# The input's chunked transfers on SyncE's queue, and a recurrence that passes its state every 128 tokens

## The chip, the cores and the metric

The kernel runs on one core of one Trainium2 chip. The metric is the device time of one execution in microseconds (us). Its engines are TensorE (PE in the profile, with its weight loads as PEld), VectorE (DVE), ScalarE (ACT), GpSimd (POOL) and SyncE (SP). SyncE, ScalarE and GpSimd each have a queue from which they hand transfers to the 16 DMA engines.

## What is computed

One forward pass of a stack of four layers over 512 tokens of width 1024: a state-space mixer (S5) and a short convolution, each followed by a SwiGLU, then dilated attention and a gated recurrence (HGRN2), each followed by a squared-ReLU MLP. The change touches the first mixer's loads and the last mixer's recurrence. Cut to those two:

```python
def s5_mixer(h, a_re, a_im, log_step, b_re, b_im, c_re, c_im, d, w_out):
    u = h.reshape(bsz, seqlen, 64, 16)              # 64 groups of 16 channels, 64 complex states each
    abr, abi = mag * cos(li * dt), mag * sin(li * dt)
    ...
    _, _, xr, xi = lax.associative_scan(_ssm_combine, (a_r, a_i, bu_re, bu_im), axis=1)
    y = einsum('ghp,blgp->blgh', c_re, xr) - einsum('ghp,blgp->blgh', c_im, xi)
    ...

def hgrn2_mixer(x, w_in, w_out, norm_g, lb):        # 8 heads of 128, chunks of C = 64 tokens
    q, key, log_f, v = chunks(q, K), chunks(key, K), chunks(log_f, K), chunks(v, V)
    b = cumsum(log_f, axis=3)
    q_dec, k_dec = q * exp(b), key * exp(-b)
    a = where(causal, einsum('bhcid,bhcjd->bhcij', q_dec, k_dec), 0.0)
    o_intra = einsum('bhcij,bhcje->bhcie', a, v)
    b_last = b[:, :, :, -1:, :]
    kv = einsum('bhcjd,bhcje->bhcde', key * exp(b_last - b), v)
    # state_{c+1} = exp(b_last_c) * state_c + kv_c ; states[c] is the state before chunk c
    o_inter = einsum('bhcid,cbhde->bhcie', q_dec, states)
    o = o_intra + o_inter                           # then a norm over each head, and a projection
```

## The kernel before

Activations lie transposed: `xT` holds 8 blocks of 128 channels by 512 tokens. A large product is the sum of three float32r products (`whi*hhi`, `whi*hlo`, `wlo*hhi`: L832 to L834 over 512 tokens, L1567 to L1569 for `v`); ScalarE makes `whi` from each loaded weight tile (L785) and VectorE `wlo` (L786). These products fill TensorE for most of the run. The order of the instructions on each engine is set when the program is built, by a scheduler that looks at the dependences and at its own estimate of each duration; so a change in one place can shift the instructions around it. Each engine then runs its list in that order and waits where an operand is late.

**The start.** `s5()` builds the first mixer's tables. ScalarE first issues the transfers of constants, of the mixer's `b` and `c` (`crow`, L182) and of `x` (L185: two transfers of 1 MB each, in which every second 128-channel block of 8 consecutive tokens goes to one partition). SyncE issues the loads of `w_ada`, 1 MB each (L232, three buffers; 20 in this stage), from which TensorE computes the modulation vectors (L239). What the tables need: VectorE derives an angle `t1y` and a magnitude; ScalarE takes its sine and cosine (`sn` L431, `cs` L433); VectorE makes the powers `pw_re`, `pw_im`; TensorE transposes `crow` (L553) and ScalarE copies it to `c` (L554); GpSimd multiplies powers and `c` into output tables `ft` (L539 to L541), and later makes `sr`, `d` and two of the intermediates `w1t` (L517). `ORDER`, a string, gives the order in which these steps are handed to the scheduler: `A` is one modulation load with its products, `K` is `setup`, `Q` the sum of squares of `x`. The first large products start at about 203 us.

**The recurrence.** `hgrn_pair(b, first)` does two heads; four pairs follow each other. Its three products are handed out before the two heads' own steps. For a head, VectorE scans the log decay (L1581), ScalarE takes three exponentials, and VectorE makes `qd` (L1587), `kd` (L1592) and the key `kk` scaled to the chunk's end (L1597). TensorE transposes `kk` (L1600), ScalarE copies it to `kt` (L1602), and TensorE makes the four 128x128 score blocks (L1605), of which VectorE keeps the causal part inside each 64-token chunk (L1607). The loop over eight chunks of 64 tokens then adds for each its scores times `v` (L1615, once per two chunks), the state times `qd` (L1617) and the chunk's `kt` times `v` (L1620, which reads 64 of the 128 partitions); VectorE updates the state `hst` in between (L1625). A plain float32 product takes two matrix instructions, so the profile counts two for each (112 for L1620's 56, x8 for four of L1605); the transposes count one. A norm over the head follows (L1628 to L1636).

## Time and profile before

| | us |
|---|---|
| median of 3 runs | 2822.16 |
| lowest and highest | 2821.14, 2823.73 |
| the profiled execution, device time | 2826.84 |
| its span, first to last instruction | 2825.1 |

The profile is of one execution, whose own time is 1.74 us above its span. Each row of a timeline gives a start in us from the span's first instruction and the time it took; "ACTq" and "SPq" are the queues of ScalarE and SyncE, whose rows are the issuing of transfers. A matrix instruction's own duration contains the depth of the pipeline, so what one costs in a row of them is the distance from its start to the next one's.

### The profile page before, as it was taken

The numbers are of one execution on the slowest core, as the hardware profiler recorded it, in microseconds if no ns is written. First come the engines' busy times: TensorE is split into PE (matmuls) and PEld (weight loads), VectorE is DVE, ScalarE is ACT, GpSimd is POOL, SyncE is SP. The second block draws the span as 40 slices with busy tenths as digits, with TensorE's granted clock in tenths as the row PEclk, the third lists the DMA queues.
The fourth block names the chain that finished last, engine by engine and source line by source line (L and its number), as shares of the span: only waits on it lengthen the run. The fifth ranks groups of instructions, "written<-read, shape, count | busy, mean of one in ns | idle before, by whom it ended". The sixth has DMA issues, their size and how long they took to land.

```text
span 2825.1 us, 37880 instructions
## 1 busy us (share of the span) xinstructions
PE 2750.9 (97%) x15516; PEld 2308.2 (82%) x15516; DVE 1570.5 (56%) x2819; ACT 1081.8 (38%) x1872; POOL 127.3 (5%) x122
## 2 busy tenths in 40 slices
PE   5899999999999999999999999999999999999998
PEld 3568978889788888898888888888888888988887
DVE  7867755547455333475545555754437656744435
ACT  4553422224233222253434434442324676532221
POOL 6520000000000000000000000000000000000000
PEclk9989999999999999999999999999999999999999
DMA  8446445433323232343323333133223212223221
GB/s 217 145 130 222 151 147 164 149 119 104 98 97 105 80 103 94 108 117 93 102 75 98 97 87 87 46 103 100 91 79 110 90 46 75 76 90 101 87 82 60
DMA packets 300866, 298.40 MB, mean 106 GB/s; under 512 B 9732, under 2 KB 287108, under 8 KB 300692
## 3 DMA queue, kind: packets, MB, share of 16 engines
q1 hardware_dynamic: 288532, 277.27, 31.2%
q10 hardware_dynamic: 9824, 12.34, 1.9%
q0 software_dynamic: 2336, 6.36, 1.0%
q8 instruction: 122, 2.00, 0.3%
q14 instruction: 52, 0.43, 0.0%
HBM read 278.90 MB, written 2.10 MB: 99 GB/s over the span
## 4 chain that ended last, share of the span: by engine, by line
PE 91%; ACT 3%; DVE 3%; POOL 2%; issue 1%; ACTq 1%; DMA 0%; SPq 0%; DVEq 0%; POOLq 0%
PE ps_mm L832 25%; PE ps_mm L833 24%; PE ps_mm L834 24%; PE ps_mm L845 2%; PE ps_mm L846 2%; PE ps_mm L847 2%; PE ps_sc L1300 1%; PE ps_pt L1327 1%; PE ps_kv L1620 1%; PE ps_b L670 1%; POOL ft L541 1%; POOL ft L540 1%; PE ps_mm L1202 1%; PE ps_mm L1204 1%; PE ps_mm L1203 1%
## 5 line engine op out<-in xcount | busy, mean ns | idle before, releaser
L832 PE MATMUL ps_mm<-hhi,whi 128*128 128x512 f32 (+1 forms) x2064 | 797.5, 386 | 0.0
L833 PE MATMUL ps_mm<-hlo,whi 128*128 128x512 f32 (+1 forms) x2064 | 791.5, 383 | 0.4 <-DVE hlo L357 0.4
L834 PE MATMUL ps_mm<-hhi,wlo 128*128 128x512 f32 (+1 forms) x2064 | 790.6, 383 | 0.2 <-DVE wlo L786 0.2
L785 ACT CAST whi<-raw 128x1024 fp32r<-128x1024 f32 (+1 forms) x428 | 413.8, 990 | 824.8 <-PE ps_mm L833 637.0
L786 DVE TENSOR_TENSOR wlo<-raw,whi 128x1024 fp32r<-128x1024 f32 (+1 forms) x428 | 485.6, 1151 | 390.3 <-ACT whi L785 358.7
L832 PEld LDWEIGHTS ps_mm<-hhi,whi 128*128 128x128 f32 x2064 | 387.5, 188 | 84.9 <-issue 3.1
L834 PEld LDWEIGHTS ps_mm<-hhi,wlo 128*128 128x128 f32 x2064 | 387.3, 188 | 83.0 <-DVE wlo L786 0.6
L833 PEld LDWEIGHTS ps_mm<-hlo,whi 128*128 128x128 f32 x2064 | 387.7, 188 | 80.4 <-DVE hlo L357 0.9
L833 PE MATMUL ps_mm<-hidl,whi 128*128 128x512 f32 (+1 forms) x1184 | 421.1, 356 | 0.3 <-DVE hidl L357 0.3
L832 PE MATMUL ps_mm<-hidh,whi 128*128 128x512 f32 (+1 forms) x1184 | 420.3, 355 | 0.4 <-ACT hidh L356 0.4
L834 PE MATMUL ps_mm<-hidh,wlo 128*128 128x512 f32 (+1 forms) x1184 | 420.4, 355 | 0.0
L833 PEld LDWEIGHTS ps_mm<-hidl,whi 128*128 128x128 f32 x1184 | 223.5, 189 | 32.1 <-DVE hidl L357 0.5
L832 PEld LDWEIGHTS ps_mm<-hidh,whi 128*128 128x128 f32 x1184 | 223.3, 189 | 32.2 <-ACT hidh L356 0.8
L834 PEld LDWEIGHTS ps_mm<-hidh,wlo 128*128 128x128 f32 x1184 | 223.5, 189 | 31.0
L1151 DVE TENSOR_TENSOR xT<-xT,ps_mm 128x512 f32<-128x512 f32 (+1 forms) x144 | 78.6, 552 | 133.9 <-PE ps_mm L834 132.6
L846 PE MATMUL ps_mm<-hhi,wlo 128*128 128x256 f32 x448 | 124.1, 279 | 0.0
L847 PE MATMUL ps_mm<-hlo,whi 128*128 128x256 f32 x448 | 123.8, 279 | 0.4 <-DVE hlo L357 0.4
L845 PE MATMUL ps_mm<-hhi,whi 128*128 128x256 f32 x448 | 123.3, 280 | 0.7 <-ACT hq L1546 0.6
L356 ACT CAST hidh<-silu 128x512 fp32r<-128x512 f32 (+1 forms) x124 | 68.9, 565 | 129.2 <-DVE silu L978 86.3
L939 DVE SCALAR_TENSOR_TENSOR xT<-ps_mm,mods,xT 128x512 f32<-128x512 f32 (+1 forms) x104 | 64.8, 626 | 93.6 <-PE ps_mm L834 93.3
L277 DVE SCALAR_TENSOR_TENSOR ada_acc<-raw,c_act,ada_acc 128x256 f32<-128x256 f32 x196 | 93.6, 483 | 4.9
L1251 POOL DMA_DIRECT2D qsw<-qc x48 | 23.4, 492 | 1583.7 <-ACT qc L1240 1569.5
(403 smaller groups left out, 3379.5 us busy)
## 6 DMA issues: line engine op xcount, KB each, us to landing
raw<-in_w_ada_dram SPq DMA_DIRECT2D x48, 1024.0 KB, 5.4
raw<-in_w_ffn_in_dram SPq DMA_DIRECT2D x44, 1024.0 KB, 5.1
raw<-in_ffn_w_up_dram SPq DMA_DIRECT2D x32, 1024.0 KB, 5.5
raw<-in_attn_w_in_dram SPq DMA_DIRECT2D x48, 512.0 KB, 5.2
raw<-in_ffn_w_down_dram SPq DMA_DIRECT2D x32, 768.0 KB, 4.3
raw<-in_w_ffn_out_dram SPq DMA_DIRECT2D x24, 768.0 KB, 4.3
raw<-in_conv_w_in_dram SPq DMA_DIRECT2D x12, 1024.0 KB, 5.3
raw<-in_attn_w_in_dram SPq DMA_DIRECT2D x12, 1024.0 KB, 5.1
```

The lines of the kernel that those rows point to most:

```text
L277: V.scalar_tensor_tensor(ac, raw[:, k, :], c_act[:, k:k + 1], ac, op0=OP.mult, op1=OP.add)
L356: A.copy(hi, src)
L785: A.copy(hi[:, sl], raw[:, sl])
L786: V.tensor_tensor(lo[:, sl], raw[:, sl], hi[:, sl].bitcast(F32), op=OP.subtract)
L832: T.matmul(ps[:, 0:n], hi[:, k, cs], h, start=(k == 0), stop=False)
L833: T.matmul(ps[:, 0:n], hi[:, k, cs], l, start=False, stop=False)
L834: T.matmul(ps[:, 0:n], lo[:, k, cs], h, start=False, stop=(k == nk - 1))
L845: T.matmul(p[:, 0:n], hi[:, k, cs], h, start=(k == 0), stop=False)
L846: T.matmul(p[:, 0:n], lo[:, k, cs], h, start=False, stop=False)
L847: T.matmul(p[:, 0:n], hi[:, k, cs], l, start=False, stop=(k == nk - 1))
L939: V.scalar_tensor_tensor(x, ps, gcol[:, m:m + 1], x, op0=OP.mult, op1=OP.add)
L1151: V.tensor_tensor(x, x, ps, op=OP.add)
```

## The change

The two transfers of `x` move out of the straight list at the head of the program into `load_chunks`, which `setup` (step `K0` of `ORDER`, after two `A` steps) calls, and SyncE issues them instead of ScalarE. In the recurrence the state is passed every 128 tokens. `join0` and `join1` hold, for each 128 tokens, the decay over its second half, two ones, and the decay over its first half; with them `kk` is scaled on to the end of the 128 tokens (`kl`) and `qd` back to their beginning (`qf`). The scores between the two halves come from an extra product of 64x64 (`kk` of the first half with `qd` of the second), which overwrites a quarter of each score block, and the mask keeps all of `qi <= kj`. What is left of the loop: three `kv` products over 128 partitions each into one bank, three state updates, four score products and three state products over 128 columns.

```diff
--- before.py
+++ after.py
@@ -58,7 +58,7 @@
     ct["selA"] = np.concatenate([(qi == 4 * np.arange(32)[None] + r).astype(f) for r in range(4)], 1)
     ct["qbm"] = (qi // 32 == np.arange(4)[None]).astype(f)
     ct["selB"] = np.concatenate([(kj == 4 * (qi % 32) + r).astype(f) for r in range(4)], 1)
-    tril = ((qi // 64 == kj // 64) & (qi <= kj)).astype(np.int32)
+    tril = (qi <= kj).astype(np.int32)
     ct["tri"] = tril.view(f)
     ct["rst"] = one * (np.arange(512) % 64 != 0).astype(f)[None]
     offs, cols, o = {}, [], 0
@@ -181,9 +181,12 @@
     for i, nm in enumerate(("ssm_c_re", "ssm_c_im")):
         nc.scalar.dma_start(crow[:, :, i, :], dap(a[nm], 0, [[64, 128], [64 * 128, 8], [1, 64]]))
 
-    for s in range(2):
-        nc.scalar.dma_start(xc[64 * s:64 * s + 64].rearrange("p l i j -> p (l i) j"),
-                            dap(a["x"], s * 128, [[8 * D, 64], [256, 32], [1, 128]]))
+    def load_chunks():
+
+        for s in range(2):
+            nc.sync.dma_start(xc[64 * s:64 * s + 64].rearrange("p l i j -> p (l i) j"),
+                              dap(a["x"], s * 128, [[8 * D, 64], [256, 32], [1, 128]]))
+
     nc.gpsimd.dma_start(drow, dap(a["ssm_d"], 0, [[0, 16], [16, 64], [1, 16]]))
 
     ident = C("ident")
@@ -567,6 +570,7 @@
 
 
         def setup(_):
+            load_chunks()
 
             P.memset(X, 0.0)
             P.tensor_tensor(X[0:16], drow, C("e")[0:16, None, :].to_broadcast([16, 64, 16]), op=OP.mult)
@@ -1532,10 +1536,20 @@
         t = hp.tile([128, 4, 128], F32, name=f"aT{i}", bufs=1)
         P.memset(t, 0.0)
         aT.append(t)
+
+    joins = []
+    for i in range(2):
+        t = hp.tile([128, 4, 4], F32, name=f"join{i}", bufs=1)
+        P.memset(t, 1.0)
+        joins.append(t)
     load_consts(hp, "tri", "rst", bufs=1)
     tri = C("tri").bitcast(I32)
     rst = C("rst")
     hid = {}
+
+    def nt_tile(shape):
+        t = sm.tile([128, 2, 256], F32, name="nt", tag="nt", bufs=3).rearrange("p k t -> p (k t)")
+        return t if len(shape) == 2 else t.rearrange("p (c i) -> p c i", c=shape[1])
 
     def hgrn_pair(b, first):
         nonlocal psG
@@ -1580,9 +1594,11 @@
             bb = t.rearrange("p (c i) -> p c i", c=8)
             V.tensor_tensor_scan(bf, rst, t, 0.0, op0=OP.mult, op1=OP.add)
             ex = hp.tile([128, S], F32, name="hx", bufs=2)
-            dec = hp.tile([128, 8], F32, name="hdec")
+            jn = joins[m % 2]
+            be = t.rearrange("p (q f i) -> p q f i", q=4, f=2)
             A.activation(ex, bf, AF.Exp)
-            A.activation(dec, bb[:, :, 63], AF.Exp)
+            A.activation(jn[:, :, 0], be[:, :, 1, 63], AF.Exp)
+            A.activation(jn[:, :, 3], be[:, :, 0, 63], AF.Exp)
             qd = qs[:, s]
             V.tensor_tensor(qd, qs[:, s], ex, op=OP.mult)
             ex2 = hp.tile([128, S], F32, name="hx", bufs=2)
@@ -1590,40 +1606,50 @@
             V.tensor_scalar(ke[:, s], ke[:, s], olb[:, m:m + 1], None, op0=OP.mult)
             kd = ex2
             V.tensor_tensor(kd, ke[:, s], ex2, op=OP.mult)
-            ex3 = hp.tile([128, 8, 64], F32, name="hx", bufs=2)
+            ex3 = nt_tile([128, 8, 64])
             V.tensor_tensor(ex3, bb[:, :, 63:64].to_broadcast([128, 8, 64]), bb, op=OP.subtract)
             A.activation(ex3, ex3, AF.Exp)
             kk = ex3.rearrange("p c i -> p (c i)")
             V.tensor_tensor(kk, kk, ke[:, s], op=OP.mult)
+
+            def joined(dst, src, c0):
+                h4 = lambda x: x.rearrange("p (q f i) -> p q f i", q=4, f=2)
+                V.tensor_tensor(h4(dst), h4(src), jn[:, :, c0:c0 + 2, None].to_broadcast([128, 4, 2, 64]), op=OP.mult)
+
+
+            kl = ke[:, s]
+            joined(kl, kk, 0)
+            qf = nt_tile([128, S])
+            joined(qf, qd, 2)
+            dec = hp.tile([128, 4], F32, name="hdec")
+            V.tensor_tensor(dec, jn[:, :, 0], jn[:, :, 3], op=OP.mult)
             kps = pst("ka", (128, 4, 128))
             for t_ in range(4):
-                T.transpose(kps[:, t_], kk[:, nat_tile(t_)], ident)
-            kt = ke[:, s].rearrange("p (q e) -> p q e", q=4)
-            A.copy(kt, kps)
+                T.transpose(kps[:, t_], kl[:, nat_tile(t_)], ident)
             aps = pst("ka", (128, 4, 128))
             for t_ in range(4):
                 T.matmul(aps[:, t_], kd[:, nat_tile(t_)], qd[:, nat_tile(t_)], start=True, stop=True)
+                o = t_ * 128
+                T.matmul(aps[0:64, t_, 64:128], kk[:, o:o + 64], qd[:, o + 64:o + 128], start=True, stop=True)
+            kt = ke[:, s].rearrange("p (q e) -> p q e", q=4)
+            A.copy(kt, kps)
             aa = aT[m % 2]
             V.copy_predicated(aa, tri[:, None, :].to_broadcast([128, 4, 128]), aps)
             es = slice(s * 128, s * 128 + 128)
+            kv = pst("kv")[:, 0:384].rearrange("p (q e) -> p q e", q=3)
+            for t_ in range(3):
+                T.matmul(kv[:, t_], kt[:, t_], v[:, t_, es], start=True, stop=True)
+            sts = hp.tile([128, 3, 128], F32, name="hst", bufs=1)
+            for t_ in range(3):
+                if t_ == 0:
+                    V.tensor_copy(sts[:, 0], kv[:, 0])
+                else:
+                    V.scalar_tensor_tensor(sts[:, t_], sts[:, t_ - 1], dec[:, t_:t_ + 1], kv[:, t_], op0=OP.mult, op1=OP.add)
             ops = pst("ho", (128, 4, 128))
-            st = None
-            for c in range(8):
-                t_, hf = c // 2, c % 2
-                rows = slice(64 * hf, 64 * hf + 64)
-                if hf == 0:
-                    T.matmul(ops[:, t_], v[:, t_, es], aa[:, t_], start=True, stop=False)
-                if c:
-                    T.matmul(ops[:, t_, rows], st, qd[:, c * 64:c * 64 + 64], start=False, stop=(hf == 1))
-                if c < 7:
-                    kv = pst("kv")[:, 0:128]
-                    T.matmul(kv, kt[rows, t_], v[rows, t_, es], start=True, stop=True)
-                    ns = hp.tile([128, 128], F32, name="hst", bufs=3)
-                    if st is None:
-                        V.tensor_copy(ns, kv)
-                    else:
-                        V.scalar_tensor_tensor(ns, st, dec[:, c:c + 1], kv, op0=OP.mult, op1=OP.add)
-                    st = ns
+            for t_ in range(4):
+                T.matmul(ops[:, t_], v[:, t_, es], aa[:, t_], start=True, stop=(t_ == 0))
+                if t_:
+                    T.matmul(ops[:, t_], sts[:, t_ - 1], qf[:, nat_tile(t_)], start=False, stop=True)
             ot = sg[:, s]
             A.copy(ot, ops.rearrange("p q t -> p (q t)"))
             sq = hp.tile([128, S], F32, name="hx", bufs=2)
```

On SyncE's list the rows that follow the six small loads are these before (`raw` is a buffer of `w_ada`, `TT` a table that is filled from `X`):

```order
L158 DMA vrow_82<-in_c_dram 8x128
L158 DMA vrow_82<-in_norm_g_dram 16x128
L158 DMA vrow_82<-in_b_ada_dram 96x128
L232 DMA raw<-in_w_ada_dram 128x8x256 x13
L665 DMA TT_255<-X 16x256
L232 DMA raw<-in_w_ada_dram 128x8x256
L665 DMA TT_254<-X 16x256
L665 DMA TT_254<-X 32x256
L665 DMA TT_254<-X 48x256
L665 DMA TT_254<-X 64x256
```

and in the changed kernel these, where the two transfers of `x` stand behind two of `w_ada`, and the first full group of `TT` stands behind eleven of `w_ada` instead of fourteen:

```order
L158 DMA vrow_82<-in_c_dram 8x128
L158 DMA vrow_82<-in_norm_g_dram 16x128
L158 DMA vrow_82<-in_b_ada_dram 96x128
L235 DMA raw<-in_w_ada_dram 128x8x256 x2
L187 DMA xT<-in_x_dram 64x32x128 x2
L235 DMA raw<-in_w_ada_dram 128x8x256 x9
L669 DMA TT_252<-X 16x256
L669 DMA TT_252<-X 32x256
L669 DMA TT_252<-X 48x256
L669 DMA TT_252<-X 64x256
L669 DMA TT_252<-X 80x256
L669 DMA TT_252<-X 96x256
```

On ScalarE's list the first instructions that are not transfers stand before like this (`vcol` holds small vectors, `c_act` the activated condition, `IC` an identity):

```order
L182 DMA crow<-in_ssm_c_im_dram 128x8x64
L185 DMA xT<-in_x_dram 64x32x128 x2
L166 ACT_TABLE_LOAD
L166 COPY vcol_123<-ps_a 128x120
L431 ACT_TABLE_LOAD
L431 ACTIVATE sn<-t1y 128x64
L388 ACT_TABLE_LOAD
L388 ACTIVATE c_act<-vcol_123 128x8
L432 ACTIVATE ab<-t1y 128x64
L574 COPY IC_256<-cst_ident 128x8x128
L433 ACTIVATE cs<-ab,cst_sws 128x64
```

In the changed kernel the `x` row is gone, and the rest keeps its order:

```order
L182 DMA crow<-in_ssm_c_im_dram 128x8x64
L166 ACT_TABLE_LOAD
L166 COPY vcol_121<-ps_a 128x120
L434 ACT_TABLE_LOAD
L434 ACTIVATE sn<-t1y 128x64
L391 ACT_TABLE_LOAD
L391 ACTIVATE c_act<-vcol_121 128x8
L435 ACTIVATE ab<-t1y 128x64
L578 COPY IC_254<-cst_ident 128x8x128
L436 ACTIVATE cs<-ab,cst_sws 128x64
```

On TensorE's list the first head of the recurrence begins like this before (`ps_ka` are transposes and scores, `ps_kv` the products for the state, `ps_ho` the output, `ps_mm` the large products of the next pair):

```order
L1600 MATMUL ps_ka<-cst_ident,hx 128x128 x4
L1605 MATMUL ps_ka<-hq,hx 128x128 x4
L832 MATMUL ps_mm<-hhi,whi 128x512
L833 MATMUL ps_mm<-hlo,whi 128x512
L834 MATMUL ps_mm<-hhi,wlo 128x512
L1620 MATMUL ps_kv<-hv,hk 128x128
L832 MATMUL ps_mm<-hhi,whi 128x512
L833 MATMUL ps_mm<-hlo,whi 128x512
L834 MATMUL ps_mm<-hhi,wlo 128x512
L832 MATMUL ps_mm<-hhi,whi 128x512
L833 MATMUL ps_mm<-hlo,whi 128x512
L1615 MATMUL ps_ho<-aT_17301,hv 128x128
```

In the changed kernel the scores alternate with the 64x64 products, the three `kv` stand together, and one large product stands between scores and `kv` where there were three:

```order
L1628 MATMUL ps_ka<-cst_ident,hk 128x128 x4
L1631 MATMUL ps_ka<-hq,hx 128x128
L1633 MATMUL ps_ka<-hq,nt 64x64
L1631 MATMUL ps_ka<-hq,hx 128x128
L1633 MATMUL ps_ka<-hq,nt 64x64
L1631 MATMUL ps_ka<-hq,hx 128x128
L1633 MATMUL ps_ka<-hq,nt 64x64
L1631 MATMUL ps_ka<-hq,hx 128x128
L1633 MATMUL ps_ka<-hq,nt 64x64
L836 MATMUL ps_mm<-hhi,whi 128x512
L1641 MATMUL ps_kv<-hv,hk 128x128 x3
```

Between the transposes of a pair's first head and those of its second there are 66 large products of `ps_mm` before and 26 in the changed kernel; the others stand behind the second head (30 before, 70 now), since the next pair's products are as many as they were.

## Rows read from the trace of the kernel before

**Rows 1.** The page: the span, and the chain that ended last by engine.

```profile
span 2825.1 us, 37880 instructions
...
PE 91%; ACT 3%; DVE 3%; POOL 2%; issue 1%; ACTq 1%; DMA 0%; SPq 0%; DVEq 0%; POOLq 0%
```

**Rows 2.** Chain that ended last, first 90 us: start, us, what.

```profile
22.60 1.28 ACT L166
...
32.38 0.34 DVE pw_re L424
...
83.81 1.98 POOL w1t L517
```

**Rows 3.** Timeline of ScalarE's queue: start, us; x2 merges two instructions.

```profile
6.88 1.80 ACTq L182 DMA_DIRECT2D crow<-in_ssm_c_im_dram  x1
...
8.72 13.85 ACTq L185 DMA_DIRECT2D xT<-in_x_dram  x2
```

**Rows 4.** DMA issues, first 140 us: KB each, median us from issue to landing.

```profile
xT<-in_x_dram ACTq DMA_DIRECT2D x2, 1024.0 KB, 20.9
```

**Rows 5.** Timeline of the start on VectorE, TensorE, ScalarE and GpSimd.

```profile
14.43 0.19 DVE L420 TENSOR_SCALAR t1y<-t1y 128x64 f32<-128x64 f32 x1
...
23.42 1.30 PE L553 MATMUL ps_a<-cst_ident,crow 128*128 128x128 f32 x5 [12.90 <-DMA crow<-in_ssm_c_im_dram]
...
25.46 0.26 ACT L431 ACTIVATE sn<-t1y 128x64 f32<-128x64 f32 x1
...
31.54 1.27 ACT L554 ACTIVATE c<-ps_a,cst_sws 128x512 f32<-128x512 f32 x2
...
32.86 9.91 POOL L539 TENSOR_TENSOR ft<-c,pw_re 128x512 f32<-128x512 f32 x8 [5.36 <-DVE tq L424]
```

**Rows 6.** Busy time of each engine by stretch; PEclk is the granted clock.

```profile
100.00:200.00 100.00, 86.00 (x655) 62.65 (x654) 74.04 (x91) 56.87 (x118) 40.96 (x29) 0.85 0.36 118
...
170.00:180.00 10.00, 10.00 (x52) 8.19 (x53) 2.58 (x4) 5.48 (x8) 3.19 (x3) 0.52 0.01 3
...
2199.00:2431.00 232.00, 225.95 (x1386) 193.78 (x1387) 135.18 (x243) 151.69 (x216) 0.00 (x0) 1.00 0.19 60
```

**Rows 7.** Timeline of TensorE in the first recurrent head: start, us.

```profile
2223.65 0.66 PE L1600 MATMUL ps_ka<-cst_ident,hx 128*128 128x128 f32 x4 [1.39 <-DVE hx L1597]
...
2224.14 1.06 PE L1605 MATMUL ps_ka<-hq,hx 128*128 128x128 f32 x8
...
2224.96 0.48 PE L832 MATMUL ps_mm<-hhi,whi 128*128 128x512 f32 x1
...
2229.68 0.33 PE L1617 MATMUL ps_ho<-hq,hst 128*128 128x64 f32 x2
...
2229.93 0.48 PE L1620 MATMUL ps_kv<-hv,hk 64*128 64x128 f32 x2
...
2230.35 0.50 PE L832 MATMUL ps_mm<-hhi,whi 128*128 128x512 f32 x1
...
2230.68 0.40 PE L833 MATMUL ps_mm<-hlo,whi 128*128 128x512 f32 x1
...
2230.92 0.39 PE L834 MATMUL ps_mm<-hhi,wlo 128*128 128x512 f32 x1
...
2231.82 0.49 PE L1615 MATMUL ps_ho<-aT,hv 128*128 128x128 f32 x2
...
2232.07 0.48 PE L832 MATMUL ps_mm<-hhi,whi 128*128 128x512 f32 x1
```

**Rows 8.** Line L1620: what ended TensorE's idle time (us, times).

```profile
  ACT hk L1602: 5.0, 6
```

**Rows 9.** VectorE groups, 2199 to 2431 us: xcount | busy us, mean ns | idle.

```profile
L786 DVE TENSOR_TENSOR wlo<-raw,whi 128x1024 fp32r<-128x1024 f32 x19 | 22.8, 1216 | 1.5 <-ACT whi L785 1.5
...
L1625 DVE SCALAR_TENSOR_TENSOR hst<-hst,hdec,ps_kv 128x128 f32<-128x128 f32 x48 | 16.6, 347 | 36.1 <-PE ps_kv L1620 35.7
...
L1592 DVE TENSOR_TENSOR hx<-hk,hx 128x512 f32<-128x512 f32 x8 | 5.5, 692 | 2.8 <-ACT hx L1589 2.8
```


## The prediction

> **What bounds the kernel now.** I read the page first. The chain that ended last lies on TensorE for 91% of the span [rows 1]; there, time goes only if TensorE's own work shrinks or something that it waits for comes earlier. The change touches two places, so I read each by itself.
>
> The start: the chain of waits runs for its first 32 us over ScalarE's queue, then VectorE, then GpSimd until 85.8 us [rows 2]. ScalarE does no work before 22.60 us, because it is issuing: the two transfers of `x` hold it from 8.72 for 13.85 us [rows 3]. `t1y`, which the sine needs, had been ready at 14.62 us, and the sine ran at 25.46 [rows 5]. The powers that follow from it end at 32.72 [rows 2], and GpSimd, which has waited 5.36 us, begins `ft` at 32.86 [rows 5] and is not idle again before its first `w1t` ends at 85.79 [rows 2].
>
> The recurrence: from 2199 to 2431 us TensorE is busy 225.95 of 232.00 us, VectorE 135.18 and ScalarE 151.69 [rows 6]. VectorE waits there 35.7 us for `kv` products [rows 9], but nobody waits for VectorE in turn: large products of the next pair fill TensorE's time. So it is a stage full of TensorE work, about 6 us idle, 5.0 of them before a first `kv`, until ScalarE has copied `kt` [rows 8]. What counts is how much TensorE work goes, and whether enough filling stays between the waits.
>
> **The start, step by step.** ScalarE is free at 8.68 us (6.88 + 1.80 [rows 3]) instead of 22.57. Two table loads of 1.28 [rows 2] and a small copy are over by 11.6, so the sine starts when `t1y` is there, at 14.62. From the start of the sine to the end of the powers it took 32.72 - 25.46 = 7.26 us; that gives 21.9. But `ft` also needs `c`, the copied transposes of `crow`. TensorE began these at 23.42 us, after 12.90 us of waiting for `crow` itself [rows 5], which has nothing to do with ScalarE's stall. If `crow` lands when it did, four of the eight transposes (five took 1.30) end at 24.5, half of the copy pair (1.27 for two) at 25.2, and GpSimd starts there: 32.86 - 25.2 = **7.7 us** earlier. Were `crow` no limit, it would be 32.86 - 21.9 = 10.9, the upper bound. I take 7.7, since the transfer is the same on the same queue and no `x` is queued behind it any more.
>
> What pays for it: SyncE now issues `x` behind two loads of `w_ada`, and if that takes 13.85 us there too, SyncE is at it from about 8 to 22 us, and the third `w_ada` load goes out then. Its products stood before the first tables; in the new order on TensorE seven table products stand ahead of them, and those need the same powers, so this wait is covered; without the cover TensorE's list would stand still until the load lands. `x` itself took 20.9 us from issue to landing [rows 4]: from about 8 us that is 29, or 36 if its time starts when its issuing ends. Its first reader, the sum of squares, stands on ScalarE behind the copies of `c` and of its swapped form, and its result is needed only after the first tables. The first full group of `TT` now stands ahead of the last nine `w_ada` loads on SyncE instead of the last six, and waits for `X`; three loads thus come later relative to the tables, and their products stand in TensorE's list between steps of the mixer. I take 1 us off for that and leave **6.7 us**. The stretch from 100 to 200 us is not one engine's (TensorE 86%, VectorE 74%), and its granted clock averages 0.85, in one stretch 0.52, near the lower of its two levels (1.2 and 2.4 GHz) [rows 6]. Its instructions are in a new order; a 10 us stretch at the other level is worth up to 5 us either way. For the range the start gives between a loss of 5 and a gain of 10.9.
>
> Here the Trainium skill speaks against the change (DMA: Bandwidth & Descriptors, section Issuing engines are not separate DMA queues): transfers of all issuing engines run on the same 16 DMA engines, and another issuer saves only the issuing, usually small beside the transfer. The trace does not agree that it is small here: 13.85 us of issuing beside 20.9 to landing [rows 3, 4]. By the rule the start would give about nothing.
>
> **The recurrence, step by step.** Costs are distances from start to start [rows 7]. One L1617 (64 columns) costs 2229.93 - 2229.68 = 0.25 us, one L1620 (64 rows) 0.42, one L1615 (128 rows, 128 columns) 0.25, and four L1605 in a row 0.82. A large product costs 0.24, but 0.33 when it follows plain float32 ones, so each change costs 0.09.
>
> Removed in each of 8 heads: seven L1617 and seven L1620, 7 x 0.25 + 7 x 0.42 = 4.69 us. Added: three `kv` over 128 rows, in a row, at L1605's rate: 3 x 0.22 = 0.66; three state products over 128 columns at L1615's 0.25: 0.75; four 64x64 products. The trace has none of these; the nearest is L1617, also 64 columns wide, 0.25 each, 1.00 together. It could be half an L1605, 0.11, or L1620's 0.42. So 4.69 - 2.41 = 2.28, times 8: 18.2 us (22.7 to 12.8 for the two bounds of the 64x64 product). The scores no longer stand in a row: 0.05 more for each of 32, 1.4 us lost. Where TensorE changed to a large product about eleven times a head it now does so about six times: 5 x 0.09 x 8 = 3.6 us gained. Sum: 20.4 us of TensorE time.
>
> The Trainium skill has a rule that would price `kv` otherwise (TensorE: Matmul & The Clock Gate, section Why this matters for your kernels): a product over few rows takes as long as one over 128. The rows differ, 0.42 over 64 rows and 0.25 over 128 [rows 7]. If the rule held and 0.42 came from where `kv` stands, the 24 new ones would cost 0.2 more each, and the sum would be 4.8 us smaller.
>
> On VectorE a head loses four updates and gains two scalings: 4 x 0.35 = 1.4 out, 2 x 0.69 = 1.4 in [rows 9]. That is no work, but one scaling now lies between `kk` and the transposes, and the filling has moved: only 26 large products stand between a pair's two sets of transposes instead of 66. Does the second head's `kl` come in time? TensorE needs about 12.3 us between them: 0.49 for the transposes, 1.9 for scores and 64x64, 0.66, 1.75 for state and value products, about 0.8 for the norm's small ones at L1605's rate, 26 x 0.24, 0.5 for changes. VectorE has in its list in between five `wlo` at 1.22, seven steps of 128x512 at 0.69 and three of 128x128 at 0.35: 12.0 us. That is no margin, and the norm's chain stands among these steps. I charge 1 us of new waiting to each of 4 pairs (0 to 3 for the range): 20.4 - 4 = **16.4 us**. The wait before the first `kv` stays as it is: one large product and four 64x64 (1.2 us) stand where three large ones (0.7 us) covered ScalarE's copy. For the range, 64x64 at 0.42 and 3 us per pair leave 3 us, 0.11 and no wait give 25.
>
> Sum: 6.7 + 16.4 = 23.1 us off the profiled execution's 2826.84, so 2803.7 for one like it; that execution stands 4.7 us above the median of the runs, 2822.16, to which the forecast refers: **2799 us**.
>
> **Rivals.**
> A: the start gives nothing, since ScalarE's issuing was not the last thing missing. If `x`, moved ahead of the third `w_ada` load, keeps `crow` back in the shared DMA engines until about 31 us, `c` comes at 33 and GpSimd starts as before. For it: TensorE waited for `crow` until 23.42 already. Against it: in place of `x` SyncE had 1 MB of `w_ada` there. 2822.2 - 16.4 = 2806. The Trainium skill's rule on issuing would come out there too.
> B: the recurrence gives little: waits of 3 us and more per pair, or 64x64 products at 0.42, leave 3 to 8 us. With the start 2808 to 2813.
> C, the other side: the pair's second head. If its `kl` comes later than TensorE's other work allows by more than 8 us in each of 4 pairs (23.1 + 4 + 5.6 = 32.7 to be eaten), the kernel is slower; at 9 us 2831. For it: VectorE's list there takes as long as TensorE's. Against it: it would have to be wrong by two thirds.
> D: nothing measurable, both terms near their lower ends: 2817 to 2827.
>
> **How the numbers follow.** About 0.2%, 5.6 us, is what a measurement of this kernel tells from no change. Forecast with both terms 0.62, A 0.14, B 0.12, C 0.05, D 0.07. Forecast and A are faster, and B almost wholly; so faster 0.87, same 0.08, slower 0.05. The range goes from 2788 (start 9, recurrence 25) to 2814 (start nothing, recurrence 8) and leaves out C, D and the tails. Both signs do not share the chance, so no second range is needed.
>
> **What the new profile would show.** Right: the sine at 14.6 us, `ft` starting near 25, the first `w1t` near 78, the first large product 6 to 7 us earlier than now (about 203 us); in the recurrence the stage shorter by 16, `kv` at about 0.22 from start to start, TensorE idle under 12 us there. Wrong: TensorE waiting long for `crow`, or for a `w_ada` load behind `TT`; `ft` starting on time but the first large product not; the second set of transposes of each pair ended by VectorE's `kl` for several us; the 64x64 products at 0.4.

## The result, and the profile after

| | before | after |
|---|---|---|
| median, us | 2822.69 (4 runs) | 2803.14 (4 runs, 2802.42 to 2803.93) |
| ratio, 95% interval | | 0.9931 (0.9914 to 0.9948) |
| the profiled execution, and its span | 2826.84, 2825.1 | 2802.42, 2800.6 |

The change takes off 0.69%, 19.5 us (0.52 to 0.86%). The forecast was 2799, 4 us lower, and its range holds the result. But the two halves did not do what their terms said: the start gave nothing, the recurrence more than its 16.4 us.

In the changed kernel lines move by 3 to 35: the states products of the first mixer are L674 (L670 before), its output tables L542 to L544, the `w_ada` products L242 (L239). In the recurrence the transposes are L1628, scores L1631, the 64x64 products L1633, `kv` L1641, scores times `v` L1650, state products L1652.

First the page of the changed kernel: its span, and the chain that ended last by engine (answers to [rows 1]).

```profile
span 2800.6 us, 37693 instructions
...
PE 91%; DVE 5%; ACT 2%; issue 1%; DMA 1%; POOL 0%; SPq 0%; DVEq 0%; ACTq 0%; POOLq 0%
```

The timeline of its start (answers to [rows 3, 5]).

```profile
7.94 8.21 SPq L187 DMA_DIRECT2D xT<-in_x_dram  x2
...
15.21 0.19 DVE L423 TENSOR_SCALAR t1y<-t1y 128x64 f32<-128x64 f32 x1
15.44 0.26 ACT L434 ACTIVATE sn<-t1y 128x64 f32<-128x64 f32 x1 [4.03 <-DVE t1y L423]
...
20.95 1.94 PE L556 MATMUL ps_a<-cst_ident,crow 128*128 128x128 f32 x8 [9.28 <-DMA crow<-in_ssm_c_im_dram]
22.08 0.69 ACT L557 ACTIVATE c<-ps_a,cst_sws 128x512 f32<-128x512 f32 x1 [0.79 <-PE ps_a L556]
23.43 3.60 POOL L542 TENSOR_TENSOR ft<-c,pw_re 128x512 f32<-128x512 f32 x3 [4.22 <-DVE qi L427]
...
72.93 3.00 POOL L520 TENSOR_TENSOR w1t<-b,pw_im 128x1024 f32<-128x1024 f32 x1
...
197.54 0.79 PE L836 MATMUL ps_mm<-hhi,whi 128*128 128x512 f32 x1
```

The head start is there: the sine 10.0 us earlier, GpSimd's `ft` 9.4 (23.43 for 32.86 [rows 5]), its first `w1t` 10.9 (72.93 for 83.81 [rows 2]). Yet the first large product starts at 197.54, where the timeline of the kernel before has it at 197.06 (not at about 203 us, as was written ahead of the result):

```profile
197.06 0.51 PE L832 MATMUL ps_mm<-hhi,whi 128*128 128x512 f32 x1
```

All of it is lost between 73 and 197 us.

In the recurrence, the timeline of TensorE in the first head (answers to [rows 7]; starts carry the cost), and what it waited for there (total, times, longest), first after, then before.

```profile
2219.26 0.65 PE L1628 MATMUL ps_ka<-cst_ident,hk 128*128 128x128 f32 x4
2219.75 0.39 PE L1631 MATMUL ps_ka<-hq,hx 128*128 128x128 f32 x2
2220.07 0.33 PE L1633 MATMUL ps_ka<-hq,nt 128*64 128x64 f32 x2
2220.33 0.49 PE L1631 MATMUL ps_ka<-hq,hx 128*128 128x128 f32 x2
2220.75 0.33 PE L1633 MATMUL ps_ka<-hq,nt 128*64 128x64 f32 x2
2221.00 0.49 PE L1631 MATMUL ps_ka<-hq,hx 128*128 128x128 f32 x2
...
2222.86 0.94 PE L1641 MATMUL ps_kv<-hv,hk 128*128 128x128 f32 x6
2223.55 0.48 PE L837 MATMUL ps_mm<-hlo,whi 128*128 128x512 f32 x1
...
2225.79 0.71 PE L1650 MATMUL ps_ho<-aT,hv 128*128 128x128 f32 x4 [1.30 <-DVE aT L1637]
2226.34 0.39 PE L1652 MATMUL ps_ho<-nt,hst 128*128 128x128 f32 x2
2226.56 0.39 PE L1650 MATMUL ps_ho<-aT,hv 128*128 128x128 f32 x2
```

```profile
PE ps_ho L1650 <- DVE aT L1637: 1.9, 2, 1.3
PE ps_st L340 <- DVE zsum L336: 1.0, 1, 1.0
PE ps_kv L1641 <- ACT hk L1635: 0.6, 1, 0.6
```

```profile
PE ps_ka L1600 <- DVE hx L1597: 3.0, 2, 1.6
PE ps_kv L1620 <- ACT hk L1602: 1.8, 2, 1.4
```

Three `kv` take 0.69 us (2223.55 - 2222.86), a state product 0.22, a 64x64 product 0.26 (2220.33 - 2220.07), but a score 0.42 (2220.75 - 2220.33) where four in a row took 0.82. Nothing there waits for `kl` (L1628). From ScalarE's first step of the recurrence (2199.21 before, 2196.22 after) to the end of the span it is 625.9 us before and 604.4 after: 21.4 less. In the three profiled executions with the old recurrence (before, experiments 1 and 10) this stretch takes 625.3 to 626.2 us, in the seven with the new one as it stands (after, experiments 2 to 6 and 9) 604.4 to 605.9: 20.8 less on average.

The two profiled executions are 24.5 us apart, more than the 19.5 of the medians. Besides these 21.4, 3.5 us lie between the first large product and the recurrence, where TensorE's list is the same and where the executions took 1998.7 to 2002.2 us. So a few microseconds between two single executions say nothing unless they are read by stage.

### The profile page after: what moved, and what is told of

The parts are those of the page before. It is cut to its first block, busy times and chain, and to the rows that moved or that the text cites. A ratio compares the mean times of both kernels' runs of the same rounds, so it can differ in the third digit from the quotient of the medians.

```text
span 2800.6 us, 37693 instructions
## 1 busy us (share of the span) xinstructions
PE 2727.4 (97%) x15452; PEld 2287.7 (82%) x15452; DVE 1571.2 (56%) x2811; ACT 1064.8 (38%) x1866; POOL 124.5 (4%) x124
## 4 chain that ended last, share of the span: by engine, by line
PE 91%; DVE 5%; ACT 2%; issue 1%; DMA 1%; POOL 0%; SPq 0%; DVEq 0%; ACTq 0%; POOLq 0%
PE ps_mm L836 25%; PE ps_mm L837 24%; PE ps_mm L838 24%; PE ps_mm L849 2%; PE ps_mm L850 2%; PE ps_mm L851 2%; PE ps_sc L1304 1%; PE ps_pt L1331 1%; PE ps_b L674 1%; PE ps_mm L1206 1%; PE ps_mm L1208 1%; PE ps_st L324 1%; PE ps_mm L1207 1%; PE ps_pv L1349 0%; PE ps_pv L1352 0%
```

## The experiments

All ratios are to the kernel before, measured beside each experiment; 0.1% is 2.8 us. The table has starts from each profiled execution's timeline in us: `ft`, the last 32 states instructions (L674), the first large product, the time between these two, and how many `w_ada` matrix instructions (L242; 16 to a group) start in that time. Each is one execution: in the five whose start has the same list of instructions (after, 1, 7, 8, 11) the last states products begin at 161.1 to 165.7 us and the first large product at 195.8 to 200.2, mean 197.9, while the time between stays at 33.8 to 34.7. Their `ft` starts at 21.9 to 25.0, mean 23.3. In the two with the start of the kernel before (before, 2) the means are 31.5, 167.5 and 196.4. So the lead is 8.2 us at `ft`, 4.1 at the last states products, and at the first large product the new start is 1.5 us behind.

| | `ft` | last states | first large | between | `w_ada` there | median, us | ratio (95%) |
|---|---|---|---|---|---|---|---|
| before | 32.86 | 167.80 | 197.06 | 29.3 | 22 | 2822.69 | |
| after | 23.43 | 162.87 | 197.54 | 34.7 | 54 | 2803.14 | 0.9931 (0.9914 to 0.9948) |
| 1 start only | 24.99 | 165.65 | 200.19 | 34.5 | 54 | 2825.25 | 1.0003 (0.9995 to 1.0012) |
| 2 recurrence only | 30.19 | 167.26 | 195.81 | 28.6 | 22 | 2805.58 | 0.9932 (0.9920 to 0.9945) |
| 3 `x` after three loads | 24.54 | 165.47 | 198.25 | 32.8 | 54 | 2803.86 | 0.9933 (0.9919 to 0.9946) |
| 4 `x` on GpSimd | 30.38 | 171.24 | 199.23 | 28.0 | 16 | 2807.43 | 0.9942 (0.9929 to 0.9954) |
| 5 groups earlier | 27.06 | 174.71 | 205.69 | 31.0 | 16 | 2809.87 | 0.9938 (0.9925 to 0.9951) |
| 6 `x` after one load | 24.41 | 165.51 | 193.41 | 27.9 | 16 | 2800.65 | 0.9908 (0.9892 to 0.9923) |
| 7 `kl` late | 23.77 | 165.01 | 199.67 | 34.7 | 54 | 2815.31 | 0.9961 (0.9948 to 0.9975) |
| 8 half of `kv` | 21.87 | 161.08 | 195.77 | 34.7 | 54 | 2808.36 | 0.9940 (0.9926 to 0.9953) |
| 9 after, 16 groups | 22.19 | 160.27 | 190.23 | 30.0 | 0 | 2800.67 | 0.9913 (0.9890 to 0.9936) |
| 10 before, 16 groups | 31.48 | 166.86 | 192.87 | 26.0 | 0 | 2821.88 | 0.9991 (0.9980 to 1.0001) |
| 11 scores in a row | 22.46 | 162.48 | 196.23 | 33.8 | 54 | 2802.63 | 0.9912 (0.9898 to 0.9926) |
| 12 both | 25.82 | 167.21 | 195.16 | 28.0 | 16 | 2797.88 | 0.9896 (0.9879 to 0.9913) |

### 1 and 2: each half alone

Experiment 1 is the kernel before with the two hunks on `x` only:

```diff
-    for s in range(2):
-        nc.scalar.dma_start(xc[64 * s:64 * s + 64].rearrange("p l i j -> p (l i) j"),
+    def load_chunks():
...
+            nc.sync.dma_start(xc[64 * s:64 * s + 64].rearrange("p l i j -> p (l i) j"),
...
         def setup(_):
+            load_chunks()
```

> The kernel before with the move of x alone; the recurrence stays as it was. Theory (the start's gain is lost again, because the third group of w_ada products now stands behind seven table products in TensorE's list and the modulation comes late): ft starts near 23.3 us, but the first large product within 1.5 us of 197.1, and the time is 2822 us, within 3. Rival (the start gives what was predicted and the recurrence less): first large product near 190.5, time 2815.5.

Experiment 2 is the changed kernel with these two hunks taken back:

```diff
-    def load_chunks():
...
+    for s in range(2):
+        nc.scalar.dma_start(xc[64 * s:64 * s + 64].rearrange("p l i j -> p (l i) j"),
...
         def setup(_):
-            load_chunks()
```

> The changed kernel with x issued by ScalarE at the head as before; the recurrence is the new one. Theory (the recurrence gives about all of the difference, TensorE's saving without new waits): 2802 us, within 2.5, so level with the changed kernel. Rival (the recurrence gives the predicted 16.4, the start the rest): 2806. Second rival (the start costs something in the changed kernel): under 2799.

The start alone: 1.0003, so between 1.4 us less and 3.4 more; `ft` at 24.99, 7.9 us earlier than before, and still no gain. The recurrence alone: 0.9932, 19.2 us (15.5 to 22.6), all that the whole change gives. Its interval holds both 16.4 and 21, so its size is read from the traces.

### 3 to 6: where the start's gain goes

The last 32 states products, first before, then after:

```profile
167.80 7.09 PE L670 MATMUL ps_b<-U,bt 128*128 128x64 f32 x32 [4.08 <-DVE sp L424]
```

```profile
162.87 7.09 PE L674 MATMUL ps_b<-U,bt 128*128 128x64 f32 x32
```

Between the last states products and the first large one, TensorE is full in both kernels but for one wait of 1.3 to 1.6 us. Its busy time in that stretch on the `w_ada` products alone (stretch and its length, PE busy and count, PEld busy and count, granted clock, share and GB/s of the DMA engines), first before, then after:

```profile
167.80:197.06 29.26, 2.76 (x22) 0.73 (x22) 0.80 0.12 39
```

```profile
162.87:197.54 34.67, 6.19 (x55) 1.81 (x54) 0.80 0.20 63
```

And the row of the changed kernel's timeline that stands ahead of it:

```profile
161.02 1.92 PE L242 MATMUL ps_x<-raw,cz 128*32 128x256 f32 x10 [5.14 <-DVE mods L260]
```

The granted clock averages 0.80 in both. The lead over the kernel before, 4.9 us when the stretch begins, meets 32 more `w_ada` instructions: worked out from the timeline, 5.64 us from start to start instead of 2.55. The small products that belong to them (L248, L245 before) take 2.20 instead of 1.04. Together that is 4.25 of the 5.4 us by which the stretch is longer. Ahead of it TensorE had stood idle for 5.14 us, since one of these groups waited for VectorE's `mods`.

Experiment 3 moves one word of `ORDER`; 4 puts `x` on GpSimd at the head of the program; 5 hands out seven groups earlier; 6 moves the same word as 3, the other way.

```diff
-    ORDER = ("A1 A1 K0 A1 A1 B0 T2 ...
+    ORDER = ("A1 A1 A1 K0 A1 B0 T2 ...      (3)
+    ORDER = ("A1 K0 A1 A1 A1 B0 T2 ...      (6)
+    ORDER = ("A1 A1 A1 K0 A1 B0 A1 A1 T2 Q0 A1 A1 Z0 O0 O4 G0 ... O3 A1 A1 A1 A1 A1 S0 "  ...      (5)
```

```diff
-            nc.sync.dma_start(xc[64 * s:64 * s + 64].rearrange("p l i j -> p (l i) j"),
+        nc.gpsimd.dma_start(xc[64 * s:64 * s + 64].rearrange("p l i j -> p (l i) j"),
```

> The changed kernel with x issued by SyncE after three w_ada loads instead of two, so that the products of the third stand ahead of the first table products again. Theory (that group's place loses the start's gain): TensorE's third group under 40 us instead of 48.9, first states product 4 to 6 us earlier than 84.5, first large product near 192, time 2798. Rival (the place of that group decides nothing; VectorE's full list from 23 to 80 us does): first large product within 1.5 us of 197.5, time 2803.

> The changed kernel with x issued by GpSimd at the head instead of SyncE; neither ScalarE nor SyncE issues it, and the w_ada loads are ahead of nothing but themselves. Theory (order and issuing of w_ada lose the start's gain): ft starts at 23 to 25 us, the second half of the modulation (fourth to eighth group) is done by 66 us, first large product 190 to 193, time 2797. Rival (what SyncE issues is not what costs): first large product within 1.5 us of 197.5, time 2803. Second rival (GpSimd's own issuing runs past 25 us and ft starts late): first large product after 199, time 2805 or more.

> The changed kernel with another ORDER: seven of the twenty w_ada groups are handed to the scheduler earlier, so that 19 of them instead of 16.6 stand ahead of the last states product of the first mixer in TensorE's list. Theory (TensorE has no idle time from there to the first large product, 31.0 us in the changed kernel against 26.6 before, since more w_ada groups are left; they eat the lead that ft had): first large product 193 to 194 us, time 2799. Rival (another limit, VectorE's list or the granted clock): first large product within 1 us of 197.5, time 2803.

> The changed kernel with x issued after one w_ada load instead of two; by its order 19 groups stand ahead of the last states product. Theory (the groups left for the end eat the lead): first large product 193 to 194 us, time 2799. Rival: within 1 us of 197.5, time 2803.

Experiment 3 refutes its theory: the third group was done at 31 us, and the first large product came at 198.25, for 54 instructions were still left at the end. Experiment 6 leaves 16: the time between is 27.9 us (28.0 in experiment 12, which has the same start), the first large product comes at 193.4 (195.2) against a mean of 197.9, and the ratio is 0.9908 against 0.9931. The intervals overlap, so it is the traces that speak for 3 to 4 us, although a single start scatters by 4; the firmer figure is the time between, 6.5 us shorter than the mean of the five, of which about 3 go since the last states products start later (165.5 and 167.2 against a mean of 163.4). Experiment 5 also leaves 16 and gains nothing: there the last states products start only at 174.71. The sum of squares of `x` is late there, 49.1 us (41.2 in the changed kernel), but so it is in experiment 3 (46.8), whose last states products start at 165.47; what holds them in experiment 5 stays open. So the number of groups left is one limit, and when the states products can start is another.

Experiment 4 hit its second rival, though not by GpSimd's issuing, which took 2.36 us. The timeline shows what held `ft` back:

```profile
1.28 2.36 POOL L185 DMA_DIRECT2D xT<-in_x_dram  x2 [0.84 <-POOLq L1727]
...
11.76 0.39 ACTq L182 DMA_DIRECT2D crow<-in_ssm_c_re_dram  x1
...
28.49 1.94 PE L553 MATMUL ps_a<-cst_ident,crow 128*128 128x128 f32 x8 [10.21 <-DMA crow<-in_ssm_c_im_dram]
```

`crow` comes 7.5 us later than in the changed kernel (20.95). With `x` in front, the loads of the other queues land later: 256 KB of `b` that ScalarE issues at 3.17 us (2.92 in the changed kernel) take 11.9 us to landing instead of 5.6.

```profile
brow<-in_ssm_b_im_dram ACTq DMA_DIRECT2D x1, 256.0 KB, 11.9
```

ScalarE's queue waits for one of these early loads before it issues `crow`, at 11.76 instead of 7.50 us: that is 4.3 of the 7.5, the rest is the longer way from issue to use. That is the mechanism of the prediction's rival A, a load kept back on the shared DMA engines; in the change itself it did not act.

### 9 and 10: without four groups

Both kernels without the last four groups, whose columns of the modulation are then zero:

```diff
+        if n >= 16:
+            if n == 19:
+                V.memset(mods[:, layer, 32:48], 0.0)
+            return
         b = ADA0[n]
```

> The changed kernel without the last four of the twenty w_ada groups of the first stage (their loads and products are left out, the modulation columns that they make are zero). In the changed kernel 3.4 of these groups stood in TensorE's list behind the start of the last states products. Theory (these groups fill TensorE's list there and eat the lead of 4.9 us that the last states products still have): from the last states products to the first large product 26 to 28 us instead of 34.7, first large product near 190, time 2796. Rival (something else holds the first large product): within 2 us of 197.5, time 2802.

> The kernel before without the same four w_ada groups; only 1.4 of them stood behind the start of its last states products. Theory: from the last states products to the first large product 26 to 28 us instead of 29.3, first large product near 195, 4 to 5 us later than in the changed kernel without them, time 2 us less than the kernel before. Rival (the groups cost both kernels the same): first large products of the two within 1.5 us of each other.

The first large product comes 7.3 us earlier in the changed kernel, 4.2 in the one before, and 2.6 us of the lead now reach it (190.23 against 192.87; the ratios, 0.9913 and 0.9991, lie 0.0009 further apart than 0.9931 and 1, which is 2.5 us). That is less than the 4 to 5 expected, and not clear of noise by itself: the ratios' intervals are wider, and single starts scatter by 4 us. The time between scatters by less than 1 us; without the groups it is 4.7 us shorter in the changed kernel and 3.3 in the one before, 30.0 and 26.0 us, where 26 to 28 had been expected of both. So of 6.6 us at the last states products 4.0 are lost behind them all the same. The timeline of TensorE in experiment 9 shows to what:

```profile
178.72 0.29 PE L718 MATMUL ps_c<-ft,sp 128*64 128x128 f32 x1 [0.63 <-DVE sp L431]
183.35 0.29 PE L718 MATMUL ps_c<-ft,sp 128*64 128x128 f32 x1 [2.37 <-DVE sp L431]
```

With the groups gone TensorE waits 3.0 us for VectorE's `sp`, the scanned states (0.3 in experiment 10). Most of the remainder is TensorE's own steps, 2.2 us more at a granted clock of 0.77 against 0.80. So the `w_ada` groups are the first limit there, and VectorE's steps on the states stand some 3 us behind it.

### 7 and 8: the recurrence's waits and `kv`

```diff
-            joined(kl, kk, 0)
+            for _ in range(5):
+                joined(kl, kk, 0)
```

> The changed kernel with the scaling that makes kl done five times (same values): four more VectorE steps of 0.69 us, 2.75 us, ahead of each head's transposes. Theory (the place of the transposes is planned for when kl is ready, large products of the next pair fill the rest, and only little of it is paid): under 3 us more, 2803 to 2806, TensorE idle in the recurrence under 8 us. Rival (kl ends 0.1 to 0.7 us ahead of its transposes, there is no cover, and each second head pays 2 us or more): 2811 to 2814.

```diff
-                T.matmul(kv[:, t_], kt[:, t_], v[:, t_, es], start=True, stop=True)
+                T.matmul(kv[:, t_], kt[0:64, t_], v[0:64, t_, es], start=True, stop=True)
```

> The changed kernel with each kv product over the first 64 of its 128 tokens; half of the tokens is left out of the state. Theory (a product over 64 rows in a row of its like costs what one over 128 does, and the 0.42 us of the kernel before came from where it stood): 0.20 to 0.26 us from start to start, time 2803 within 1.5. Rival (64 rows cost 0.42 wherever they stand): 24 products x 0.2 = 4.8 us more, 2808.

Experiment 7 went to the rival: 0.9961, 8.5 us more than the changed kernel. What TensorE waited for in its recurrence:

```profile
PE ps_ka L1629 <- DVE hk L1617: 7.6, 4, 3.5
```

```profile
2229.80 1.12 PE L1629 MATMUL ps_ka<-cst_ident,hk 128*128 128x128 f32 x4 [3.47 <-DVE hk L1617]
...
2286.00 0.66 PE L1629 MATMUL ps_ka<-cst_ident,hk 128*128 128x128 f32 x4 [1.26 <-DVE hk L1617]
```

All four waits are at a pair's first head. Second heads wait nowhere: more large products now stand ahead of their transposes (21.3 us between the first pair's two sets, 14.3 in the changed kernel). So `kl` is on the path, but not at the head that the prediction feared for. These 7.6 us are not the whole account: other waits fell, so that TensorE waits 5.0 us more than in the changed kernel, and its work in the new order takes 3.7 us more, the scores 1.3 of them.

Experiment 8, the timeline of TensorE in the first head:

```profile
2224.21 0.93 PE L1641 MATMUL ps_kv<-hv,hk 64*128 64x128 f32 x6
2225.07 0.50 PE L837 MATMUL ps_mm<-hlo,whi 128*128 128x512 f32 x1
```

Three `kv` over 64 rows take 0.86 us, 0.29 each: a little over the theory's 0.26, and not the rival's 0.42. Inside the row the step from instruction to instruction is 0.11 us, as over 128 rows; the two outermost steps are 0.21 and 0.20. In the changed kernel, over 128 rows in the same place, the first is 0.21 as well and the last 0.03. In the kernel before, L1620 stood alone between products over 128 rows, and its two instructions took 0.21 and 0.20: that is the 0.42 of [rows 7], both ends paid by each. The time rose by 2.5 us by the ratios, whose intervals overlap, and the recurrence by 3.0 by the trace (607.4 for 604.4). `kv` itself costs 6.9 us instead of 5.3 over all heads (distances as above, 48 instructions).

### 11 and 12: scores in a row

```diff
                 T.matmul(aps[:, t_], kd[:, nat_tile(t_)], qd[:, nat_tile(t_)], start=True, stop=True)
+            for t_ in range(4):
                 o = t_ * 128
                 T.matmul(aps[0:64, t_, 64:128], kk[:, o:o + 64], qd[:, o + 64:o + 128], start=True, stop=True)
```

> The changed kernel with each head's four 128x128 score products handed out first and the four 64x64 products behind them, instead of in turns. Theory (each change between products whose stationary operands differ in shape costs TensorE about 0.1 us on either side, and in the changed kernel there are seven more per head): four scores 0.92 us instead of 1.56, four 64x64 0.6 instead of 1.04; 1.05 us x 8 heads = 8.4 us of TensorE work, time 2795. Rival (what a head saves is waited for again, at VectorE's copy of the scores and its kl, since there is no cover): under 3 us, 2801 to 2803.

> The same with x issued after one w_ada load instead of two. Theory (the 2 to 3 us at the start and the 8.4 us of the recurrence add up): first large product 193.4, time 2792. Rival (only one of them shows): 2795 or more.

The first head of experiment 11, and the waits of its recurrence:

```profile
2222.04 1.06 PE L1631 MATMUL ps_ka<-hq,hx 128*128 128x128 f32 x8
2223.03 0.68 PE L1634 MATMUL ps_ka<-hq,nt 128*64 128x64 f32 x8
2223.64 0.50 PE L836 MATMUL ps_mm<-hhi,whi 128*128 128x512 f32 x1
```

```profile
PE ps_kv L1642 <- ACT hk L1636: 3.3, 4, 1.6
```

Scores take 0.99 us a head and the 64x64 products 0.61, 1.6 where it was 2.6. That is the 1 us a head of the theory, 8.0 in all. But other products cost 2.9 us more where they now stand, so TensorE's work falls by 5.1 us, and it waits 3.3 us more, 2.7 of them for ScalarE's `kt`, which the longer scores had covered. From the first step of the recurrence to the end 602.7 us are left of 604.4: by the trace the rival's size, though the wait is for ScalarE's copy and not for VectorE's steps that the rival named. By the ratios (0.9912 for 0.9931) it could be 5 us, but the intervals overlap. Both edits together (12) give 0.9896, 2797.88 us, the fastest of all, and their interval ends below that of the changed kernel; the theory's 2792 is not reached.

## Why the prediction was right, and where its steps were not

The forecast of 2799 came within 4 us, but in part by luck: the start was credited with 6.7 us that it did not give, and the recurrence with 4 to 5 us too little.

**The start, first half: right.** ScalarE freed early, the sine when `t1y` is there (15.44 for 14.6), GpSimd as soon as `c` is. In the two profiled executions `crow` landed 2.5 us earlier than before and `ft` gained 9.4 us where 7.7 had been forecast; over all executions of the two starts it is 8.2 on average, and `ft` scatters by 3 us.

**The start, second half: the step that failed.** "[T]hree loads thus come later relative to the tables, and their products stand in TensorE's list between steps of the mixer. I take 1 us off for that and leave" 6.7 us. The cost was all of the lead, 9.4 us at `ft`. It is 7.0 us when the second of the four blocks' states products start (105.52 for 112.52), 4.9 at the last block's; the first block's even start 2.4 us later than before (84.54 for 82.11). Then 54 instead of 22 `w_ada` instructions stand ahead of the first large product, and it is gone. Experiments 6, 9 and 10 show that these groups cost time there: with the groups put elsewhere or left out, the stretch is 3.3 to 6.5 us shorter. With them put elsewhere (6 and 12), the first large product comes 3.6 us earlier; with four of them left out of both kernels, it gains 3.1 us more in the changed one than in the one before. These two sizes rest on single executions. That VectorE is next shows in 9. How the first 4.5 us of the lead went, between 23 and 163 us, no experiment separates. The prediction had named this outcome: `ft` starting on time but the first large product not.

The Trainium skill (DMA: Bandwidth & Descriptors, section Issuing engines are not separate DMA queues) would have had the start give about nothing. Experiment 1 agrees with that outcome, and its premise that all issuers share the same engines fits experiment 4; but issuing was not too small to matter, since `ft` did come 9.4 us earlier.

**The recurrence, TensorE's work: right in the sum (20.4 forecast, 19.4 measured), by terms that err against each other.** Worked out from the two timelines as distances from start to start without the waits, from the recurrence's first step to the end:

| | before, us | after, us | predicted difference | measured |
|---|---|---|---|---|
| `kv` (112, 48 instructions) | 23.2 | 5.3 | -18.2 | -17.9 |
| state products (112, 48) | 13.7 | 4.8 | -8.0 | -8.9 |
| 64x64 products (64) | | 8.3 | +8.0 | +8.3 |
| scores (64) | 7.3 | 12.5 | +1.4 | +5.2 |
| scores times `v`, large products, `v` | 540.4 | 534.0 | -3.6 | -6.4 |
| all of TensorE's work | 607.6 | 588.2 | -20.4 | -19.4 |

The last row takes in the norm's small products too (0.3 us more after).

The mis-sized term is the scores: the prediction let each lose 0.05 us by no longer standing in a row, and it lost 0.16, because a 64x64 product on either side changes the shape of the stationary operand twice. The Trainium skill (TensorEngine Tiling (Array Packing), section Tiling Modes) says that changing the tiling mode drains TensorE. The trace agrees as far as it goes: 0.05 to 0.15 us on each side of a change, in [rows 7], in experiment 8 and, taken away, in 11 (1.0 us a head for six changes fewer). A first step of 0.21 us also follows a large product without any change of shape, as the `kv` over 128 rows show, so not every such step is the shape's. The rule of the Trainium skill that the prediction weighed (TensorE: Matmul & The Clock Gate, section Why this matters for your kernels), by which a product over few rows takes as long as one over 128, holds by experiment 8 in a row of its like, at 0.11 us an instruction.

**The recurrence, the new waits: wrong by 6 us.** "I charge 1 us of new waiting to each of 4 pairs." Instead TensorE waits 6.7 us from there to the end, 8.6 before. The second heads' `kl` came 0.31 to 0.65 us ahead of their transposes every time. The prediction had also misread where TensorE stood idle before: the 5.0 us of [rows 8] add the idle time of its weight loads. TensorE itself waited 1.8 us before a first `kv`, and 3.0 before the transposes of two first heads, for VectorE's `kk`. These 3.0 are gone, and the 1.8, which were to stay, fell to 0.6: ScalarE's copy lies beside 2.6 us of scores. New are 1.9 us for the masked scores (`aT`). With 19.4 of work and 1.9 of waits the recurrence gives 21.3 us by the traces, within what experiment 2 measured.

**Rivals.** A's outcome, no gain from the start, came true by another mechanism; with the larger recurrence the time came out at 2803 and not at A's 2806. B, C and D did not come. What C feared, that TensorE waits for `kl`, is near: 2.75 us more of VectorE's work per head cost 8.5 us in experiment 7, though at first heads.

## What to carry to other kernels

Here an earlier start gained only where the list of the engine that is full at the stage's end got shorter too, and not even always then (experiment 5): count what is left there in the new order, at the price of its rows, before crediting a lead. Price a short product by the neighbours that it will have, since the shape changes around it can cost as much as the product, and remember that making it cheaper takes away cover from the copy behind it.

## What was not expected of the hardware

The same two transfers of `x` held ScalarE's queue for 13.85 us [rows 3], SyncE's for 8.21 (7.14 in experiment 6) and GpSimd for 2.36; from issue to landing they took 20.9 us [rows 4] and, from GpSimd, 13.8 (the row of DMA issues of experiment 4):

```profile
xT<-in_x_dram POOLq DMA_DIRECT2D x2, 1024.0 KB, 13.8
```
